# The first norm of a trunk layer: x loaded by features and scaled by a row, in place of normalizing by tokens and transposing

## The chip, the cores and the metric

The kernel runs on one core of one Trainium2 chip. The metric is the device time of one execution in microseconds (us). The engines are TensorE (PE in the profile; its weight loads are PEld), VectorE (DVE), ScalarE (ACT) and GpSimd (POOL); SyncE (SP) issues every DMA of this kernel, and they go through one queue.

## The reference

The layer is a pre-normed stick-breaking attention and a dense SwiGLU feed-forward on x of 2048 tokens by 1024 features in float32, with shift, scale and gate worked out from a vector c. What matters here is its very first step:

```python
def rms_norm(x, g):
    y = xf * lax.rsqrt(jnp.mean(xf * xf, axis=-1, keepdims=True) + EPS)
    return (y * g.astype(jnp.float32)).astype(x.dtype)
...
h = modulate(rms_norm(x, norm_g[i, 0]), sh_m, sc_m)     # h * (1 + scale) + shift
qkv = (h @ w_qkv).reshape(b, s, 3, N_HEADS, HEAD_DIM)
```

So h of a token t and a feature d is x[t, d] * rstd[t] * gain[d] + shift[d], with one rstd a token and one gain and shift a feature.

## The kernel before

Tokens are cut into four blocks of 512 (0 to 3), features into eight groups of 128 (k = 0 to 7). Attention heads are taken in eight pairs p. TensorE needs h with features on partitions, as tiles of 128 features by 512 tokens, each split into a high and a low part in float32r (the pair `ht`), because every product is three matmuls: high by high, high by low, low by high (`mm3`, lines 169 to 171). Three such matmuls are called a slice here; a projection of one block to q, k or v of a head pair is eight slices.

The norm before, for blocks 1 to 3: `x_load` brings four tiles of 128 tokens by 1024 features. `x_square` (line 160 does the square with its sum on ScalarE) and the helper's lines 162 (mean, VectorE) and 164 (power -1/2, GpSimd) give a scale for each token. `x_scale` (line 315, VectorE) multiplies a tile of x by it. `x_turn` (line 324) turns a feature group of the four tiles on TensorE into PSUM, a group of four 128x128 transposes. `modulate` then applies gain and shift out of PSUM on ScalarE (line 334), makes the high part on VectorE (line 340) and the low part (line 342) on VectorE for blocks 1 and 2 and on GpSimd for block 3. `first_norm` (line 361 on) does this for one k, and stores two groups of h to DRAM (`h_s`, line 363) for the later head pairs. Block 0 has its own code (lines 700 to 716) and isn't changed.

The order of the work around it is written out by hand. `project` yields once a slice. `STEPS` starts with (pair 0, block 0), then (pair 1, block 0), whose results are parked in DRAM ("parked"), then (pair 0, blocks 1, 2, 3). In each step the products come in the order k (t = 1), q (t = 0), v (t = 2). While a step runs, the next block's norm is prepared: its x is loaded in the k product, its squares and scales are done in the q product (`t == 0`), its first three feature groups in the v product (slices 2, 4 and 6); the other five are done in the first slices of its own k product, three ahead of use. From slice 42 of the projections on, the attention of the first blocks runs between the slices: scores z (line 528), sigmoids on ScalarE (545, 547), scans on VectorE (557, 562), weights by a multiplication on GpSimd (569), transposes t (579), copies aT (589 on ScalarE, 595 on VectorE), and products with v (607).

Each engine works its instructions in the order written. Only the order on SyncE is left to the framework, which places each DMA by its own reckoning of time. A DMA instruction on SyncE waits for the data, for a free buffer and for the DMA eight places ahead of it; what stands behind it waits too. Tiles share rings of buffers by tag: x in `v` (7 buffers), normalized x in `kt` (7, with the keys), h in `ht` (5), the intermediate `hf` in `tmp` (4). In the text, kt and qt are the copies of a block's keys and queries, `k_park` and `q_park` the parked ones, and wr a raw projection weight.

Of the kernel before, what the change touches and what calls it, by code (L numbers as in the profile page):

```python
# [9 lines left out]
F32 = mybir.dt.float32  # L10
F32R = mybir.dt.float32r
AF = mybir.ActivationFunctionType
# [57 lines left out]

H2_STEP = 3

LAST_HELD = 30

HOW = ["aav", "avv", "avv", "avp"]


def f32(ap):
    return ap.bitcast(F32)
# [22 lines left out]
def hybrid_trunk_kernel(  # L102
    ctx: ExitStack,
    tc: tile.TileContext,
    x: bass.AP,
    c: bass.AP,
    ada_first: bass.AP,
    ada_w: bass.AP,
# [79 lines left out]
    def load_weights(p, t, tag="wraw"):  # L188
        raw = att.tile([P, KC, P], F32, name=f"wr{p}_{t}", tag=tag, bufs=BUFS[tag])
        nc.sync.dma_start(raw, wqkv[p, t])  # L190
        raws[p, t] = raw
# [105 lines left out]
            yield  # L297


    x_tiles, x_norm, x_rstd = {}, {}, {}  # L300

    def x_load(b):
        for i in range(4):
            r0 = b * BT + i * P
            xt = att.tile([P, D], F32, name=f"x{b}_{i}", tag="v", bufs=BUFS["v"])
            nc.sync.dma_start(xt, x[r0 : r0 + P])
            x_tiles[b, i] = xt

    def x_square(b, i):
        xn = att.tile([P, D], F32, name=f"xn{b}_{i}", tag="kt", bufs=BUFS["kt"])  # L310
        x_norm[b, i] = xn
        x_rstd[b, i] = rms_scale(att, x_tiles[b, i], f"n0_{b}_{i}", junk=xn)

    def x_scale(b, i):
        nc.vector.tensor_scalar(
            x_norm[b, i], x_tiles.pop((b, i)), x_rstd.pop((b, i)), None, op0=ALU.mult
        )

    def x_turn(b, k):

        pool, tag = (tps, "t") if b < 2 else (accps, "acc")
        pt = pool.tile([P, BT], F32, name=f"xT{b}_{k}", tag=tag)
        for i in range(4):
            nc.tensor.transpose(
                pt[:, i * P : (i + 1) * P], x_norm[b, i][:, k * P : (k + 1) * P], ident
            )
        return pt

    def modulate(hl, pt, which, k, name, how="aap"):

        full = att.tile([P, BT], F32, name=name, tag="tmp", bufs=BUFS["tmp"])
        gain, add = g_eff[:, which, k : k + 1], shift[:, which, k : k + 1]
        if how[0] == "a":
            nc.scalar.activation(full, pt, AF.Identity, bias=add, scale=gain)
        else:
            nc.vector.tensor_scalar(full, pt, gain, add, op0=ALU.mult, op1=ALU.add)
        if how[1] == "a":
            nc.scalar.copy(hl[:, 0], full)
        else:
            nc.vector.tensor_copy(hl[:, 0], full)  # L340
        eng = nc.gpsimd if how[2] == "p" else nc.vector
        eng.tensor_tensor(hl[:, 1], full, f32(hl[:, 0]), op=ALU.subtract)

    def h_load(p, b):
        h = []
# [39 lines left out]
    def project(at):  # L385
# [10 lines left out]
        def product(t):  # L396
            if begun:
                return first_acc[t]
            w = weights[p, t]
            if parked and t == 1:  # L400
                acc = zps.tile([P, BT], F32, name=f"pj{p}_{b}_{t}", tag="z")
            else:
                acc = accps.tile([P, BT], F32, name=f"pj{p}_{b}_{t}", tag="acc")
            ahead = b == NB - 1 and p + 1 < NPAIR
            for k in range(KC):
                if t == 1:
                    if p == 0:
                        first_norm(b, k + 3)
                    if k == 0 and nb and nb > 1:
                        x_load(nb)  # L410
                    if k == 5 and waiting:
                        waiting.pop()()
                if parked and t == 1 and k % 2 == 0:
                    nc.sync.dma_start(*stores[k // 2])
# [12 lines left out]
            return acc  # L427
# [342 lines left out]
    for q in range(4):  # L770
# [835 lines left out]
```

## Time and profile before

| | |
|---|---|
| median of 3 runs | 2851.53 us (2848.06 to 2854.43) |
| the profiled execution | 2849.01 us |
| its span in the trace | 2846.9 us |
| outside the span | 2.1 us |
| granted TensorE clock | 1.0 |
| TensorE busy | 2797.7 us, 98% |

The changed stretch is the first 150 us of the span. Rows of the profile name an instruction by the line of the code that issues it and by the tiles it writes and reads (out<-in), with buffer numbers left out. A row of a timeline has the start, the duration, the engine, and in brackets how long the engine stood idle ahead of it and who ended that wait. A matmul's row is longer than the distance to the next one, since matmuls overlap in the array; distances of starts are used for costs. In the chain of waits each row is a start, a length and what the whole execution waited for at that moment.

### The profile page before, as it was taken

To read this page: it belongs to the slowest core of one execution; us is meant where nothing else is said; L and a number is where in the kernel's file an instruction comes from. 1 tells how busy PE (TensorE), PEld (TensorE's weight loads), DVE (VectorE), ACT (ScalarE), POOL (GpSimd) and SP (SyncE) were. 2 spreads that over 40 slices of the span, in tenths; PEclk is the share of its full clock that TensorE was granted. 3 is DMA by queue.
4 is the path that set the end of the run, shared out by engine and by line. 5 is a ranking of instruction groups with operands and counts; after the bars stand their busy time and mean duration, and the time that the engine had idled before them with its cause. 6 is when DMAs were issued, how large, how long until landed. Compare 5 with 4: busy or idle time off the path is not lost.

```text
span 2846.9 us, 41792 instructions
## 1 busy us (share of the span) xinstructions
PE 2797.7 (98%) x13848; PEld 2333.6 (82%) x13848; DVE 2031.8 (71%) x2825; ACT 1629.6 (57%) x3263; POOL 1278.3 (45%) x2032
## 2 busy tenths in 40 slices
PE   7999999999999999999999999999999999999998
PEld 6788888888888888887888888888788888888887
DVE  6788898888888888888866766555775665133477
ACT  4787877788787877777645533333433333322343
POOL 1475666666576655656410122221222222544454
PEclk9999999999999999999999999999999999999999
DMA  8765546656665635546289645334463335545565
GB/s 323 276 210 168 189 153 229 211 173 231 189 208 192 207 119 179 196 132 231 88 300 310 205 137 152 122 97 162 130 176 109 112 107 163 191 142 155 180 215 193
DMA packets 239368, 516.84 MB, mean 182 GB/s; under 512 B 22320, under 2 KB 110384, under 8 KB 221488
## 3 DMA queue, kind: packets, MB, share of 16 engines
q1 hardware_dynamic: 239152, 514.18, 55.7%
q8 instruction: 109, 1.79, 0.3%
q14 instruction: 107, 0.88, 0.1%
HBM read 346.85 MB, written 118.49 MB: 163 GB/s over the span
## 4 chain that ended last, share of the span: by engine, by line
PE 88%; DVE 5%; issue 2%; ACT 2%; DMA 1%; POOL 1%; SPq 0%; DVEq 0%; POOLq 0%; ACTq 0%
PE s L169 9%; PE s L171 9%; PE s L170 9%; PE z L528 8%; PE o L607 8%; PE t L579 8%; PE pj L169 6%; PE pj L170 6%; PE pj L171 6%; PE o L171 5%; PE o L169 5%; PE o L170 5%; PE y L171 1%; PE y L169 1%; PE y L170 1%
## 5 line engine op out<-in xcount | busy, mean ns | idle before, releaser
L569 POOL TENSOR_TENSOR a<-a,w 128x512 f32<-128x512 f32 (+3 forms) x640 | 620.0, 969 | 218.0 <-DVE w L562 127.1
L562 DVE TENSOR_TENSOR_SCAN w<-z,c,begin 128x512 f32<-128x512 f32 x384 | 489.4, 1279 | 82.0 <-ACT z L547 61.4
L169 PE MATMUL s<-r,l 128*128 128x512 f32 x1232 | 481.5, 391 | 4.3 <-DVE p L1369 3.9
L171 PE MATMUL s<-r,l 128*128 128x512 f32 x1232 | 479.5, 389 | 0.0
L170 PE MATMUL s<-r,l 128*128 128x512 f32 x1232 | 479.3, 389 | 0.0
L545 ACT ACTIVATE a<-z 128x512 f32<-128x512 f32 (+3 forms) x640 | 346.8, 542 | 167.4 <-PE z L528 137.1
L607 PE MATMUL o<-aT,v 128*128 128x512 f32 (+3 forms) x1280 | 384.2, 381 | 0.1
L595 DVE TENSOR_TENSOR aT<-t,aT 128x512 fp32r<-128x512 f32 (+3 forms) x640 | 358.9, 595 | 22.6 <-ACT aT L589 21.9
L528 PE MATMUL z<-kt,qt 128*128 128x512 f32 (+3 forms) x1280 | 363.1, 365 | 0.0
L589 ACT CAST aT<-t 128x512 fp32r<-128x512 f32 (+3 forms) x640 | 314.0, 533 | 73.8 <-PE t L579 63.6
L547 ACT ACTIVATE z<-z 128x512 f32<-128x512 f32 (+3 forms) x640 | 345.3, 539 | 0.0
L1377 POOL TENSOR_TENSOR one<-p,p 128x512 f32<-128x512 f32 x44 | 71.2, 1618 | 577.4 <-issue 320.3
L169 PE MATMUL pj<-ht,w 128*128 128x512 f32 x768 | 309.8, 403 | 6.3 <-issue 1.4
L170 PE MATMUL pj<-ht,w 128*128 128x512 f32 x768 | 302.2, 393 | 1.3 <-DVE ht L715 0.7
L579 PE MATMUL t<-begin,a 128*128 128x128 f32 x2176 | 294.8, 273 | 8.5 <-DVE aT L595 7.2
L579 PEld LDWEIGHTS t<-begin,a 128*128 128x128 f32 x2176 | 255.1, 140 | 58.1 <-DVE aT L595 11.0
L171 PE MATMUL pj<-ht,w 128*128 128x512 f32 x768 | 302.0, 393 | 0.0
L169 PEld LDWEIGHTS s<-r,l 128*128 128x128 f32 x1232 | 231.2, 188 | 54.5 <-ACT l L1230 2.9
L170 PEld LDWEIGHTS s<-r,l 128*128 128x128 f32 x1232 | 231.3, 188 | 48.5 <-issue 0.5
L171 PEld LDWEIGHTS s<-r,l 128*128 128x128 f32 x1232 | 231.2, 188 | 47.9
L557 DVE TENSOR_TENSOR_SCAN w<-z,begin 128x128 f32<-128x128 f32 (+3 forms) x256 | 208.7, 818 | 74.8 <-ACT z L547 63.3
L528 PEld LDWEIGHTS z<-kt,qt 128*128 128x128 f32 x1280 | 230.2, 188 | 37.4 <-DVE w L557 0.2
(160 smaller groups left out, 4866.5 us busy)
## 6 DMA issues: line engine op xcount, KB each, us to landing
ht<-h_s SPq DMA_DIRECT2D x108, 1024.0 KB, 8.0
wi<-in_win SPq DMA_DIRECT2D x86, 512.0 KB, 4.0
qt<-qn SPq DMA_DIRECT2D x124, 256.0 KB, 4.8
ol_qt<-act_s SPq DMA_DIRECT2D x56, 512.0 KB, 3.7
act_s<-S SPq DMA_DIRECT2D x66, 256.0 KB, 4.1
br<-in_wout SPq DMA_DIRECT2D x66, 256.0 KB, 3.6
h_s<-ht SPq DMA_DIRECT2D x16, 1024.0 KB, 7.9
o_s<-os SPq DMA_DIRECT2D x128, 128.0 KB, 2.7
```

The source lines that it names most:

```text
L169: nc.tensor.matmul(acc, lhs[0], rhs[0], start=first, stop=False, **kw)
L170: nc.tensor.matmul(acc, lhs[0], rhs[1], start=False, stop=False, **kw)
L171: nc.tensor.matmul(acc, lhs[1], rhs[0], start=False, stop=last, **kw)
L528: nc.tensor.matmul(z[:, :n], q[:, e, part, r * P : (r + 1) * P], k[:, e, :n], start=part == 0, stop=part == 1,)
L545: nc.scalar.activation(a[:, :n], z[:, :n], AF.Sigmoid, scale=QK_SCALE)
L547: nc.scalar.activation(z[:, :n], z[:, :n], AF.Sigmoid, scale=-QK_SCALE)
L562: nc.vector.tensor_tensor_scan(rest[:, rev], left[:, rev], begin[:, :BT][:, rev], initial=carries[r], op0=ALU.mult, op1=ALU.bypass,)
L569: nc.gpsimd.tensor_tensor(a[:, :n], a[:, :n], rest[:, 1 : n + 1], op=ALU.mult)
L579: nc.tensor.transpose(pt[:, rb * P : (rb + 1) * P], weighed[i, rb][:, j * P : (j + 1) * P], ident)
L589: nc.scalar.copy(hl[:, 0, t0:], pt[:, t0:])
L595: nc.vector.tensor_tensor(hl[:, 1, t0:], pt[:, t0:], f32(hl[:, 0, t0:]), op=ALU.subtract)
L607: nc.tensor.matmul(acc[:, t0:], lhs, hl[:, part, t0:], start=sc == qb and j == 0 and part == 0, stop=sc == 0 and j == 3 and part == 1,)
```

## The change

A second copy of x, laid out by features (`xt`: for blocks 1 to 3, 128 partitions of features, eight groups, 512 tokens), is passed to the kernel. It is made from the input on the host, as every other input's layout is. `cols_load` brings a block's columns in four tiles of 512 KB, in buffers of tag `kt`, where the normalized x lay. The token tiles of x are still loaded, but only for the squares. `x_spread` writes each token's scale 128 times into a 128x128 corner of its x tile; `x_share` turns these four corners on TensorE, which gives a tile with the row of 512 scales on every partition, and copies it to SBUF on ScalarE. `scale_cols` multiplies a feature group by the row, even k with the gain in one instruction on VectorE, odd k without it on GpSimd. `modulate` then adds the shift: for even k ScalarE writes the high part at once and VectorE the low part; for odd k ScalarE applies gain and shift, ScalarE copies the high part, and VectorE subtracts.

The places change too. Block 1's squares move from the parked step's q product to its k product, its row stands in the second slice of the parked q product, and four of its groups are done in the parked step (`NORM_AT`), at q slices 4 and 6 and v slices 3 and 5. Blocks 2 and 3 keep their squares in the q product, and their row stands ahead of the v product. The scaling runs two groups ahead of the modulation. The text calls block 1, 2 or 3 what the code calls `b`.

```diff
+NORM_AT = {True: [(0, 4), (0, 6), (2, 3), (2, 5)], False: [(2, 2), (2, 4), (2, 6)]}
...
+    def cols_load(b):
+        for m in range(KC // 2):
+            cols = att.tile([P, 2, BT], F32, name=f"xc{b}_{m}", tag="kt", bufs=BUFS["kt"])
+            nc.sync.dma_start(cols, xt[b - 1, :, 2 * m : 2 * m + 2])
+            x_cols[b, 2 * m], x_cols[b, 2 * m + 1] = cols[:, 0], cols[:, 1]
...
     def x_square(b, i):
+        if b > 0:
+            tok = x_tiles[b, i]
+            x_rstd[b, i] = rms_scale(att, tok, f"n0_{b}_{i}", junk=tok)
+            return
...
+    def x_spread(b, i):
+        nc.vector.tensor_scalar(
+            x_tiles[b, i][:, :P], ones, x_rstd.pop((b, i)), None, op0=ALU.mult
+        )
+
+    def x_share(b):
+        pool, tag = (tps, "t") if b < 2 else (accps, "acc")
+        pt = pool.tile([P, BT], F32, name=f"xr{b}", tag=tag)
+        for i in range(4):
+            tok = x_tiles.pop((b, i))
+            nc.tensor.transpose(pt[:, i * P : (i + 1) * P], tok[:, :P], ident)
+        x_row[b] = tok[:, BT:]
+        nc.scalar.copy(x_row[b], pt)
...
+    def scale_cols(b, k):
+        u = x_cols[b, k]
+        if k % 2 == 0:
+            nc.vector.scalar_tensor_tensor(
+                u, u, g_eff[:, 0, k : k + 1], x_row[b], op0=ALU.mult, op1=ALU.mult
+            )
         else:
+            nc.gpsimd.tensor_tensor(u, u, x_row[b], op=ALU.mult)
+
+    def modulate(hl, b, k):
+        u = x_cols.pop((b, k))
+        gain, add = g_eff[:, 0, k : k + 1], shift[:, 0, k : k + 1]
+        if k % 2 == 0:
+            nc.scalar.activation(hl[:, 0], u, AF.Identity, bias=add)
+            nc.vector.scalar_tensor_tensor(
+                hl[:, 1], u, add, f32(hl[:, 0]), op0=ALU.add, op1=ALU.subtract
+            )
         else:
+            nc.scalar.activation(u, u, AF.Identity, bias=add, scale=gain)
+            nc.scalar.copy(hl[:, 0], u)
+            nc.vector.tensor_tensor(hl[:, 1], u, f32(hl[:, 0]), op=ALU.subtract)
...
-        modulate(norm_h[b][k], x_turn(b, k), 0, k, f"hf{b}_{k}", HOW[b])
+        for ahead in range(0 if k == 0 else k + 2, min(k + 3, KC)):
+            scale_cols(b, ahead)
+        modulate(norm_h[b][k], b, k)
...
-                        first_norm(b, k + 3)
+                        first_norm(b, k + (4 if b == 1 else 3))
                     if k == 0 and nb and nb > 1:
                         x_load(nb)
+                        cols_load(nb)
...
-                if t == 0 and nb:
-                    (x_square if k < 4 else x_scale)(nb, k % 4)
-                if t == 2 and k in (2, 4, 6):
-                    first_norm(nb, k // 2 - 1)
+                if t == (1 if nb == 1 else 0) and nb:
+                    if k < 4:
+                        x_square(nb, k)
+                    if 2 <= k < 6:
+                        x_spread(nb, k - 2)
+                if nb and (t, k) == ((0, 1) if nb == 1 else (2, 0)):
+                    x_share(nb)
+                if (t, k) in NORM_AT[nb == 1]:
+                    first_norm(nb, NORM_AT[nb == 1].index((t, k)))
...
             load_weights(1, 2, "v")
+            cols_load(1)
```

More of the change, by code (lines that the diff above doesn't have):

```diff
@@ L105, in hybrid_trunk_kernel @@
     x: bass.AP,
+    xt: bass.AP,
     c: bass.AP,
@@ L297, in late_modulation @@
             yield
-    x_tiles, x_norm, x_rstd = {}, {}, {}
+    x_tiles, x_norm, x_rstd, x_cols, x_row = {}, {}, {}, {}, {}
     def x_load(b):
@@ L327, in x_turn @@
         return pt
[L329 to L334, printed above, removed]
-        else:
-            nc.vector.tensor_scalar(full, pt, gain, add, op0=ALU.mult, op1=ALU.add)
-        if how[1] == "a":
-            nc.scalar.copy(hl[:, 0], full)
-        else:
-            nc.vector.tensor_copy(hl[:, 0], full)
-        eng = nc.gpsimd if how[2] == "p" else nc.vector
-        eng.tensor_tensor(hl[:, 1], full, f32(hl[:, 0]), op=ALU.subtract)
+    def scale_cols(b, k):
[4 more added lines that the diff above has]
+            )
+        else:
+            nc.gpsimd.tensor_tensor(u, u, x_row[b], op=ALU.mult)
[7 more added lines that the diff above has]
+            )
+        else:
+            nc.scalar.activation(u, u, AF.Identity, bias=add, scale=gain)
+            nc.scalar.copy(hl[:, 0], u)
+            nc.vector.tensor_tensor(hl[:, 1], u, f32(hl[:, 0]), op=ALU.subtract)
     def h_load(p, b):
@@ L1581 @@
         "x": get("x")[0],
+        "xt": get("x")[0].reshape(NB, BT, KC, P).transpose(0, 3, 2, 1)[1:],
         "c": get("c")[0].reshape(KC, P).T,
```

10 lines of the change are left out of this document (4 added, 6 removed).

## The prediction, made before the changed kernel was run

> **What bounds the kernel now.** I read the page first, then the busy time in stretches, then the chain of waits over 50 to 150 us, then TensorE and the DMA issues one by one. The page, then five stretches (time, and busy us of PE, PEld, DVE, ACT and POOL, granted clock, DMA share, GB/s):
>
> ```profile
> span 2846.9 us, 41792 instructions
> PE 2797.7 (98%) x13848; PEld 2333.6 (82%) x13848; DVE 2031.8 (71%) x2825; ACT 1629.6 (57%) x3263; POOL 1278.3 (45%) x2032
> ...
> 45.00:50.00 5.00, 4.78 (x21) 3.49 (x20) 2.52 (x4) 4.60 (x6) 0.00 (x0) 1.00 0.01 5
> ...
> 80.00:90.00 10.00, 8.92 (x42) 6.96 (x41) 4.93 (x12) 5.32 (x10) 2.89 (x5) 1.00 1.02 395
> 90.00:100.00 10.00, 9.69 (x58) 8.04 (x57) 8.05 (x14) 8.04 (x18) 2.50 (x7) 1.00 1.04 295
> 140.00:150.00 10.00, 9.82 (x55) 7.73 (x54) 9.87 (x12) 8.59 (x17) 8.64 (x11) 1.00 0.57 200
> 150.00:160.00 10.00, 10.00 (x58) 8.67 (x57) 8.64 (x13) 8.48 (x18) 8.64 (x20) 1.00 0.97 321
> ```
>
> TensorE is the bound, and from 150 us on it shows no gap. So the change is worth what it moves the end of the third new block's norm, near 150 us; I take the 2700 us behind it as shifted whole. Ahead of that TensorE has gaps, and from 80 to 100 us all DMA engines are busy (from 45 to 50 they stood still). The chain of waits (start, us, what) names who makes the gaps:
>
> ```profile
> 76.03 7.69 DMA x<-in_x
> ...
> 106.48 0.59 ACT kn L431
> 107.07 1.04 ACT xn L160 x2
> 108.11 0.37 ACT aT L589
> ```
>
> For almost 8 us the chain of the whole kernel is the load of the third block of x (rows 1024 to 1535, "block 2"); it lands at 76.03 + 7.69 = 83.72, and TensorE waits for it. At 107 us it is ScalarE, which squares block 3 and only then serves the attention (aT).
>
> **What goes from TensorE.** Starts of TensorE work:
>
> ```profile
> 58.08 0.39 PE L169 MATMUL pj<-ht,w 128*128 128x512 f32 x1
> 58.76 0.39 PE L169 MATMUL pj<-ht,w 128*128 128x512 f32 x1
> 64.20 0.70 PE L324 MATMUL xT<-begin,xn 128*128 128x128 f32 x3
> 65.32 0.48 PE L169 MATMUL pj<-ht,w 128*128 128x512 f32 x1
> 70.46 0.60 PE L324 MATMUL xT<-begin,xn 128*128 128x128 f32 x4
> 71.60 0.60 PE L324 MATMUL xT<-begin,xn 128*128 128x128 f32 x4
> 85.82 0.33 PE L324 MATMUL xT<-begin,xn 128*128 128x128 f32 x1
> 87.89 0.47 PE L169 MATMUL pj<-ht,w 128*128 128x512 f32 x1
> 109.13 0.33 PE L579 MATMUL t<-begin,a 128*128 128x128 f32 x1 [0.16 <-DVE aT L595]
> 119.40 0.66 PE L324 MATMUL xT<-begin,xn 128*128 128x128 f32 x4 [1.04 <-DVE qn L432]
> 129.83 0.33 PE L579 MATMUL t<-begin,a 128*128 128x128 f32 x1 [0.54 <-DVE aT L595]
> 135.51 0.50 PE L169 MATMUL pj<-ht,w 128*128 128x512 f32 x1 [0.92 <-ACT hf L334]
> ```
>
> A slice of three products takes 58.76 - 58.08 = 0.68 us. With a group of four transposes in front it takes 71.60 - 70.46 = 1.14, so a group costs 0.46. Of 24 groups, three come back to turn the row of scales: 21 x 0.46 = 9.7 us of pure TensorE work go. Waits before the first group of a block: block 1, 65.32 - 64.20 - 0.46 = 0.66; block 2, 87.89 - 85.82 - 0.46 = 1.61; later 1.04, 0.54 and 0.92. All of it would be 14.4 us. The question is what is late next.
>
> **What the loads do.** DMA issues (start, us of the issue, count), then issues asked for singly (KB, us to landing):
>
> ```profile
> 33.96 0.33 SPq L414 DMA_DIRECT2D h_s<-ht  x1
> 55.83 1.28 SPq L462 DMA_DIRECT2D qt<-qn  x1
> 57.15 4.20 SPq L414 DMA_DIRECT2D h_s<-ht  x3
> 65.81 0.32 SPq L457 DMA_DIRECT2D q_park<-qn  x1
> 98.66 0.45 SPq L306 DMA_DIRECT2D x<-in_x  x1
> ```
>
> ```profile
> qt<-qn SPq DMA_DIRECT2D x1, 256.0 KB, 5.8
> ...
> q_park<-qn SPq DMA_DIRECT2D x1, 512.0 KB, 6.0
> ...
> x<-in_x SPq DMA_DIRECT2D x1, 512.0 KB, 7.8
> ```
>
> The last qt piece lands at 55.83 + 5.8 = 61.6, q_park at 65.81 + 6.0 = 71.8; between them went three stores of 1 MB and two of 0.5 MB: 4 MB in 10.2 us, 2.55 us per MB. The queue works in its order.
>
> The changed program, as built, reorders it. (a) Block 1's feature columns (2 MB) are issued behind the third product's weights and land by about 50 us, in the stretch where the DMAs stood still: free. (b) The first store of block 0's h, alone at 33.96 before, now stands behind kt and qt with the other three. So from 61.6 on the queue carries 4 MB of those stores, 1 MB of parked k and q, 2 MB of block 1's first two stores, and block 2's x (2 MB): 9 MB x 2.55 = 23.0, **x of block 2 lands at 84.6**, not earlier than the 83.7 of before, although it is issued some 5 us sooner. (c) Behind it stand 2 MB of block 2's columns (+5.1 us), while two weight loads (1 MB, -2.55) move far back. So block 3's first x, which landed at 98.66 + 7.8 = 106.5, comes at 106.5 + 0.9 + 5.1 - 2.55 = **109.9**. Also moved behind more data are kt and qt of block 1; by the same count qt lands near 102 to 103, where TensorE asks for it at about 105.
>
> **Prices of the new work.** Groups, mean ns:
>
> ```profile
> L334 ACT ACTIVATE hf<-xT,shift,g_eff 128x512 f32<-128x512 f32 x24 | 18.7, 779 | 16.3 <-PE xT L324 14.7 <-ACT z L547 1.0 <-ACT hf L334 0.6
> L160 ACT ACTIVATE xn<-x 128x1024 f32<-128x1024 f32 x12 | 12.7, 1060 | 0.9 <-DMA x<-in_x 0.7
> L569 POOL TENSOR_TENSOR a<-a,w 128x512 f32<-128x512 f32 x11 | 12.1, 1097 | 5.4 <-issue 4.2 <-DVE w L562 0.8
> L164 POOL TENSOR_TENSOR n_rstd<-n_ms,mhalf 128x1 f32<-128x1 f32 x12 | 8.3, 698 | 63.9 <-DVE n_ms L162 63.9
> ```
>
> ```profile
> L651 DVE SCALAR_TENSOR_TENSOR asum<-ac,c_act,asum 128x512 f32<-128x512 f32 x23 | 17.3, 750 | 1.0 <-DMA ac<-in_ada_first 0.4
> ...
> L710 ACT CAST ht<-hf 128x512 fp32r<-128x512 f32 x8 | 5.0, 620 | 0.3
> ```
>
> VectorE's scaling and low part with a scalar: 0.75 (L651). ScalarE out of SBUF: between 0.62 (L710, no bias) and 0.78 (L334, from PSUM); I take 0.62 plain, 0.70 with gain. Spreading a scale over 128x128 lies between nothing and L651's 0.75 for four times the width; I take 0.25, and as much for a sum's readout and its mean. GpSimd's scaling: 1.10 (L569). Per block VectorE does 4 + 8 instructions of some 0.75 and four spreads, about 10 us, as before; ScalarE 4 x 0.62 + 4 x (0.70 + 0.62) + 0.62 for the row, 8.4 for 6.2; GpSimd gets 4.4 us in blocks 1 and 2, and four multiplications for eight subtractions in block 3; it idles 5.4 us ahead of the attention's multiplications here (L569), which is the room for them. ScalarE's extra 2.2 us lie beside TensorE as long as ScalarE stays under its 8.6 of 10 us.
>
> **The sum, block by block** (after against before, at the same point of TensorE's order).
>
> *Block 1.* Its squares move ahead, right behind the copy of the first values, to about 52 to 57 us (4 x 1.06 + 0.25 each), and its row is turned in the second slice of the parked q product, which begins at 58.08: a wait of 0.3 at most. Four of eight tiles are ready before the k product of block 1 starts. TensorE gains 8 x 0.46 - 0.46 + 0.66 = 3.9. The v product of block 1 began two slices and a score pair (I take a group's 0.46) ahead of 85.82, at 84.0; now at 80.1.
>
> *Block 2.* Its row is now turned ahead of that product. x lands at 84.6; then square 1.06, power 0.70, and readout, mean, spread and the last transpose at 0.25 each: 2.8, so TensorE goes on at 87.4 after **7.3 us of waiting** in place of 1.6. Two slices and the score pair later it is at 89.2 where it was at 87.89: 1.3 late. The seven groups behind (3.2) put it ahead again: block 2's k product, before at its end when ScalarE took it up at 106.48, ends at 104.6 to 107.6, the 3 us for waits on VectorE, busy 8 of 10 there already.
>
> *Block 3.* That spread doesn't matter, because ScalarE's next work in order is block 3's first square, which now waits until 109.9 with the attention's copy aT queued behind it. VectorE's low part waits for that copy, and TensorE's fourth transpose group for its bank. Before, from that square (in the chain from 107.07, behind the copy kn) to that transpose (109.13) it took 2.1; now 109.9 + 2.1 = 112.0, **2.9 late**. Behind it go eight groups (3.7) and come one (0.46). Of the later waits I let 0.54 and 0.92 go (both stand behind the casts and the affine step out of PSUM), and the 1.04 come back as a wait for the row.
>
> Sum: 2.9 - 3.7 + 0.46 - 1.46 = **-1.8 us**. The profiled execution took 2849.01 us for its span of 2846.9, so it would take 2847.2; it lay 2.5 below the median of the runs shown, 2851.53, which goes to **2849.7**.
>
> **Rivals.** (1) *The loads are in time* (for it: x is issued earlier; against it: the queue is full from 57 us on). Then all 14.4 less some 0.5 for the new row waits: -13.9, 2837.6 against that median. (2) *Only block 3's x is in time*, if kt and qt go faster beside other transfers than by my count: it needs 3 us. Then block 2's k product, taken 1.2 ahead, keeps that: -1.2 - 3.7 + 0.46 - 1.46 = -5.9, 2845.6. (3) *Slower: VectorE and GpSimd block each other.* One row each:
>
> ```profile
> 99.74 1.47 DVE L342 TENSOR_TENSOR ht<-hf,ht 128x512 fp32r<-128x512 f32 x1
> 101.57 0.69 DVE L342 TENSOR_TENSOR ht<-hf,ht 128x512 fp32r<-128x512 f32 x1
> ```
>
> ```profile
> 99.52 1.13 POOL L569 TENSOR_TENSOR a<-a,w 128x512 f32<-128x512 f32 x1 [2.28 <-issue]
> ```
>
> The same VectorE subtraction takes 0.69 alone and 1.47 beside a GpSimd multiplication that it seems to wait out: 0.78 lost. After, twelve VectorE instructions a block read two tiles, and GpSimd multiplies beside them for the norm and the attention. If each loses 0.78, that is 9.4 a block. Block 2's part is mostly swallowed by the wait for x; block 3's is not. It decides from the third of the twelve on (1.8 / 0.78 = 2.3), and with eight of them hit it adds 6.2: +4.4, 2855.9; with all, 2859.1. [...]
>
> **How the numbers follow.** Forecast 0.42, (1) 0.18, (2) 0.14, (3) 0.26. About 0.2%, 5.7 us, is what a measurement of this kernel can tell from no change. Faster by more: all of (1), 0.09 of (2), 0.03 of the forecast, 0.30. Slower by more: 0.13 of (3), where ten or more are hit, and 0.05 of the forecast, 0.18. Within: 0.52. The forecast's own range is 2846 to 2854 (3 us for the landing of x, 2 for which waits go). With (1) down to its value and (3) but for its last step of 0.8, the range is 2837 to 2858.
>
> **What would show it.** Block 2's x landing at 83.5 to 86 us, and TensorE idle for 6 to 8 us ahead of the row's four transposes near 80 to 87; the chain of waits again on that load; ScalarE's first square of block 3 waiting for its x near 107 to 110; TensorE without gaps from 150 us on. Wrong: that idle time under 3 us (then rival 1); VectorE's two-input instructions near 1.1 us on average in 90 to 150 us (rival 3); a shift that still changes behind 160 us (then something beyond these blocks moved).

## The result, and the profile after

The changed kernel took 2857.21 us (median of 15 runs, 2854.76 to 2860.46) against 2849.28 for the kernel before in the same rounds: a ratio of **1.0024, 95% interval 1.0016 to 1.0032**, some 6.8 us slower by the ratio and 7.9 between the medians. The forecast was 1.8 us faster. The time lies inside the range that was given (2837 to 2858), in its last 0.8 us and on the other side of no change; the median of before that the forecast was counted from, 2851.53, lies 2.3 above this one. The range went that far for rival 3's sake, so that it holds the time says nothing for the sum.

The page after, and the same stretches as before (time, then busy us of PE, PEld, DVE, ACT, POOL, granted clock, DMA share, GB/s), with one more behind:

```profile
span 2856.8 us, 41649 instructions
PE 2797.1 (98%) x13764; PEld 2332.0 (82%) x13764; DVE 2041.5 (71%) x2821; ACT 1638.0 (57%) x3278; POOL 1292.7 (45%) x2036
...
80.00:90.00 10.00, 3.54 (x11) 2.30 (x10) 2.83 (x10) 5.66 (x10) 3.00 (x5) 0.69 1.03 414
90.00:100.00 10.00, 9.78 (x47) 7.71 (x46) 8.68 (x11) 7.52 (x16) 5.29 (x9) 0.96 1.01 365
100.00:110.00 10.00, 6.55 (x26) 5.13 (x26) 9.93 (x11) 6.70 (x14) 5.68 (x10) 0.83 0.98 360
140.00:150.00 10.00, 6.26 (x33) 4.71 (x32) 9.41 (x11) 8.74 (x17) 5.79 (x8) 0.94 0.66 237
150.00:160.00 10.00, 10.00 (x41) 8.30 (x40) 7.21 (x11) 7.32 (x18) 7.44 (x12) 0.72 0.52 178
```

The transposes are gone from TensorE: 13764 instructions for 13848, 84 fewer, 21 groups of four. Its busy time is hardly less all the same (2797.1 us of 2797.7), since a product at the lower clock counts longer: its row is 0.63 us from 89 to 90 us, at a granted 0.50, and 0.39 from 79 to 80, at 1.00. It now has large holes: 3.5 busy us of 10 in 80 to 90, 6.3 in 140 to 150, where it had 8.9 and 9.8. New is the column of the clock: 0.69, 0.83, 0.72, where it had been 1.00 from 40 us on.

The chain of waits, and the starts of TensorE's work that end a hole (last bracket: idle time before, and who ended it):

```profile
73.37 12.15 DMA x<-in_x
...
110.41 0.59 ACT kn L473
110.99 1.05 ACT x L160 x2
...
146.18 1.21 DVE ht L376
...
148.98 0.69 DVE aT L637
```

```profile
80.19 0.39 PE L171 MATMUL pj<-ht,w 128*128 128x512 f32 x1
85.94 0.45 PE L341 MATMUL xr<-begin,x 128*128 128x128 f32 x1 [5.36 <-DVE x L331]
...
101.22 0.50 PE L170 MATMUL pj<-ht,w 128*128 128x512 f32 x1 [1.13 <-DVE ht L376]
...
104.50 0.80 PE L170 MATMUL pj<-ht,w 128*128 128x512 f32 x1 [2.32 <-DVE ht L370]
```

```profile
141.78 0.63 PE L621 MATMUL t<-begin,a 128*128 128x128 f32 x4 [0.95 <-DVE aT L637]
...
149.71 0.90 PE L621 MATMUL t<-begin,a 128*128 128x128 f32 x3 [2.75 <-DVE aT L637]
```

Three places lose time. Block 2's x lands at 73.37 + 12.15 = 85.5, and TensorE, done with the product in front at 80.4, goes on with products at 88.25. Near 100 us it waits 1.13 and 2.32 us for VectorE's low parts of block 2. At 147 us it waits 2.75 us for aT, which VectorE makes only behind two low parts of block 3 (the chain's L376 at 146.18 and what follows).

How far TensorE is behind at each place is read by setting the start of one and the same product in both traces beside each other. The table gives that shift (us; minus is ahead) at five products of the kernel before and, at 144.9, an attention transpose ahead of the last wait of block 3, all named by their start there, for every kernel of this study, with the ratio of the whole time. At 54 us nothing has changed yet but for the start: subtract it. It is 2.7 and 2.4 us in the executions of f3_x2_early and f4_block1_x2_only. From 154 us on the shift stays within 0.1 us for 150 us and more; later, single executions scatter by a microsecond or two, and the ratio decides.

| kernel | 54.2 | 81.6 | 87.9 | 106.5 | 144.9 | 154.1 | ratio, 95% interval |
|---|---|---|---|---|---|---|---|
| changed | +0.1 | -3.6 | +3.1 | +3.9 | +1.7 | +7.1 | 1.0024 (1.0016 to 1.0032) |
| e1_stores_early | +0.1 | -1.7 | +2.2 | +3.1 | +0.8 | +6.3 | 1.0019 (1.0010 to 1.0028) |
| e2_scale_on_dve | +0.1 | -3.6 | +3.6 | +3.6 | +3.7 | +7.6 | 1.0035 (1.0022 to 1.0047) |
| e6_both | +0.5 | -3.2 | -1.2 | -0.1 | +1.0 | +4.9 | 1.0015 (1.0006 to 1.0024) |
| e3_warm | 0.0 | -3.7 | +3.7 | +4.6 | +2.4 | +6.4 | 1.0023 (1.0014 to 1.0032) |
| e8_warm2 | -0.3 | -4.0 | +2.5 | +2.7 | +0.9 | +6.3 | 1.0018 (1.0009 to 1.0027) |
| e4_block1 | +0.2 | -3.5 | +3.2 | +4.4 | +4.4 | +4.4 | 1.0018 (1.0009 to 1.0027) |
| e7_blocks12 | +0.2 | -3.6 | +3.8 | +4.7 | +4.7 | +4.7 | 1.0018 (1.0009 to 1.0027) |
| e5_block3 | +0.5 | +0.5 | +0.5 | +0.5 | -0.4 | +2.3 | 1.0012 (1.0003 to 1.0021) |
| f3_x2_early | +2.7 | -0.6 | -1.8 | -1.5 | -2.7 | 0.0 | 0.9994 (0.9986 to 1.0003) |
| g1_low3_pool | 0.0 | -2.1 | -3.3 | -3.2 | -3.5 | -1.2 | 0.9994 (0.9985 to 1.0003) |
| f1_block1_x2_early | +0.5 | -2.6 | -3.9 | -3.9 | -3.9 | -3.9 | 0.9985 (0.9976 to 0.9994) |
| f2_blocks12_x2_early | +0.4 | -2.2 | -3.4 | -2.5 | -2.5 | -2.5 | 0.9989 (0.9980 to 0.9998) |
| f0_loads_only | +0.2 | +0.2 | -1.2 | -1.1 | -1.2 | -1.2 | 0.9992 (0.9983 to 1.0001) |
| f4_block1_x2_only | +2.4 | -1.4 | -1.6 | -1.6 | +3.0 | +3.0 | 1.0007 (0.9998 to 1.0016) |
| h1_no_pool_scaling | +0.2 | -3.5 | -4.7 | -4.4 | -3.4 | -1.6 | 0.9983 (0.9974 to 0.9991) |
| h2_no_dve_scaling | +0.1 | -3.6 | -4.8 | -5.5 | -6.9 | -4.6 | 0.9983 (0.9973 to 0.9992) |

The changed kernel's row tells the story: 3.6 us ahead behind block 1, near the 3.9 forecast; that and more lost to the load of block 2's x; and in block 3, where the forecast won 4.7 us, another 3.2 lost.

### The profile page after: what moved, and what is told of

Same layout as the page of the kernel before. It is cut to its first block, busy times and chain, and to the rows that moved or that the text cites. A ratio compares the mean times of both kernels' runs of the same rounds, so it can differ in the third digit from the quotient of the medians.

```text
span 2856.8 us, 41649 instructions
## 1 busy us (share of the span) xinstructions
PE 2797.1 (98%) x13764; PEld 2332.0 (82%) x13764; DVE 2041.5 (71%) x2821; ACT 1638.0 (57%) x3278; POOL 1292.7 (45%) x2036
## 4 chain that ended last, share of the span: by engine, by line
PE 86%; DVE 5%; issue 3%; ACT 2%; DMA 2%; POOL 1%; SPq 0%; DVEq 0%; POOLq 0%; ACTq 0%
PE s L169 9%; PE s L170 9%; PE s L171 9%; PE z L570 8%; PE o L649 8%; PE t L621 8%; PE pj L169 6%; PE pj L170 6%; PE pj L171 6%; PE o L171 4%; PE o L169 4%; PE o L170 4%; PE y L171 2%; PE y L169 2%; PE y L170 2%
## 5 line engine op out<-in xcount | busy, mean ns | idle before, releaser
L631 ACT CAST aT<-t 128x512 fp32r<-128x512 f32 (+3 forms) x640 | 314.0, 533 | 72.8 <-PE t L621 62.7
```

The source lines that it names most:

```text
L631: nc.scalar.copy(hl[:, 0, t0:], pt[:, t0:])
```

## The experiments

Theory A, the forecast's own: the loads decide, the rest is won. Theory B: besides, VectorE's two-input instructions lose time beside GpSimd's (for short the port, a name for durations alone: 0.66 to 0.75 us or, beside a multiplication on GpSimd, up to 1.87 in the changed kernel), and TensorE's clock halves behind long waits (0.50 granted from 104.4 to 107.8 us there, behind the wait of 2.32). Theory C came after the first four: in block 3 VectorE is as full as TensorE, so that transposes taken from TensorE win nothing there.

### The loads, first attempt, and the scaling's engine

e1_stores_early, the store loop put behind block 0's norm in place of one store every second slice of the parked k product:

```diff
+    for store in stores:
+        nc.sync.dma_start(*store)
...
-                if parked and t == 1 and k % 2 == 0:
-                    nc.sync.dma_start(*stores[k // 2])
```

> The four stores of block 0's h (4 MB) go ahead of kt and qt of block 0, into the stretch from 47 us on in which the DMA queue runs empty in the changed kernel; nothing else changes. Both theories: block 2's x lands near 77 us in place of 85.5, and TensorE's wait of 7.2 us ahead of block 2's row (80.4 to 88.1) goes but for 1 us, with the half-speed stretch behind it. Theory A (the loads are all of it): the time then falls to that of my rival 1, 0.995 to 0.997 of the kernel before. Theory B (loads, and besides VectorE and GpSimd holding each other up, and a TensorE clock that halves behind each longer wait): the waits of TensorE for VectorE in blocks 2 and 3 stay, the one near 147 us above all (2.75 us and 2.6 us of half clock behind it); 0.998 to 1.001.

It missed under both: block 2's x landed at 84.5, one us earlier. The queue in front was empty, but SP stood at the store of block 1's second pair of tiles until 72.8 us, and the loads of x are issued behind it. The shorter queue didn't help a load that was issued late. The wait at the end of block 3 stayed at 2.76.

e2_scale_on_dve, and e6_both with e1's edit as well:

```diff
-            nc.gpsimd.tensor_tensor(u, u, x_row[b], op=ALU.mult)
+            nc.vector.tensor_tensor(u, u, x_row[b], op=ALU.mult)
```

> The odd tiles of blocks 1 to 3 are multiplied by the row on VectorE in place of GpSimd; the loads are as in the changed kernel. Theory B (the port): VectorE's two-input instructions of the norm fall from a mean of 1.0 to 1.1 us in 88 to 150 us to 0.75 to 0.85 (the attention's GpSimd multiplications still meet some), four instructions of 0.7 come per block, and the wait near 147 us shrinks from 2.75 to under 1.5 us: 2 to 4 us faster than the changed kernel, 1.001 of the kernel before. Rival (VectorE is simply overloaded, GpSimd's share was a relief): VectorE gets 2.8 us more per block and the waits grow: 2 to 5 us slower than the changed kernel, 1.003 to 1.004. The wait for block 2's x stays at 7 us under both.

> Both edits: the stores of block 0's h early, and the odd tiles scaled on VectorE. Theory B: neither the wait for x nor the port's share is left, the time falls to 0.996 to 0.998 of the kernel before, and lower than with either edit alone. Rival to B (VectorE simply overloaded): the same as the stores alone or slower than that by 2 to 4 us.

VectorE's groups in the norms of blocks 2 and 3 (count, busy us, mean ns), changed kernel, then e2_scale_on_dve:

```profile
L370 DVE SCALAR_TENSOR_TENSOR ht<-xc,shift,ht 128x512 fp32r<-128x512 f32 x8 | 8.5, 1068 | 0.1
L376 DVE TENSOR_TENSOR ht<-xc,ht 128x512 fp32r<-128x512 f32 x8 | 8.4, 1046 | 1.1 <-ACT ht L375 1.1
L358 DVE SCALAR_TENSOR_TENSOR xc<-xc,g_eff,x 128x512 f32<-128x512 f32 x8 | 7.9, 1004 | 0.7 <-ACT x L343 0.7
```

```profile
L358 DVE SCALAR_TENSOR_TENSOR xc<-xc,g_eff,x 128x512 f32<-128x512 f32 x8 | 7.3, 908 | 0.7 <-ACT x L343 0.7
L370 DVE SCALAR_TENSOR_TENSOR ht<-xc,shift,ht 128x512 fp32r<-128x512 f32 x8 | 6.9, 863 | 0.0
L376 DVE TENSOR_TENSOR ht<-xc,ht 128x512 fp32r<-128x512 f32 x8 | 6.5, 813 | 0.1
L362 DVE TENSOR_TENSOR xc<-xc,x 128x512 f32<-128x512 f32 x8 | 6.4, 802 | 0.0
```

The mean fell from 24.8 / 24 = 1.03 us to 27.1 / 32 = 0.85, as theory B has it, and yet it got no faster: 1.0035 for 1.0024, with intervals that overlap, and a shift of +7.6 for +7.1. Eight more instructions outweigh what the 24 gained, VectorE's sum rises by 2.3 us, as the rival has it. With the stores early as well (e6_both) it was 1.0015, inside the interval of e1_stores_early and far from the 0.996 to 0.998 expected; there block 2's x was also issued earlier, and landed at 73.67 + 7.79 = 81.5. Neither the load nor the port was the whole cause.

### The clock

e3_warm: 22 matmuls of 512 columns ahead of the row's first transpose. e8_warm2 fills between the transposes too:

```diff
+            if b == 2:
+                for _ in range((24, 8, 0, 6)[i]):
+                    nc.tensor.matmul(
+                        pt[:, i * P :], warm[0], warm[1][:, i * P :], start=True, stop=True
+                    )
             nc.tensor.transpose(pt[:, i * P : (i + 1) * P], tok[:, :P], ident)
```

> 22 matmuls of 128x512 into the row's own bank, which the row's transposes overwrite, are put ahead of block 2's row: TensorE works through 5 of the 7.2 us that it waits there. Nothing that the output needs changes. Theory of the clock (a wait of over 2 us is followed by some 3 us at half clock): the six products behind the row keep a pitch of 0.23 us in place of 0.43, and TensorE is 1.2 us earlier at the next score product; the granted clock in 80 to 90 us rises from 0.69 to 0.95 or more. At the end of block 3 between 0 and 1.2 us of it are left. Rival (the slow pitch comes from the loads or from the port, not from the wait): the pitch stays at 0.43.

> The changed kernel, with matmuls that fill the wait for block 2's x in full: 24 of 512 columns ahead of the row's first transpose, 8 of 384 columns ahead of the second, 6 of 128 ahead of the fourth, all into columns that the transposes behind them overwrite. (With 22 ahead of the first alone, waits of 0.8, 1.0 and 0.4 us were left within 3 us, and the pitch behind them was still 0.43.) Theory of the clock: without any wait of over 0.4 us the products behind the row come at a pitch of 0.23, and TensorE is 1.0 to 1.3 us earlier at 92 us than in the changed kernel, if the filling itself ends no later than the row's data. Rival (the slow pitch is not from the idle time): 0.43 again.

The starts of the products behind the row: the changed kernel, then e8_warm2.

```profile
88.25 0.77 PE L169 MATMUL pj<-ht,w 128*128 128x512 f32 x1
...
89.67 0.63 PE L169 MATMUL pj<-ht,w 128*128 128x512 f32 x1
90.10 0.63 PE L170 MATMUL pj<-ht,w 128*128 128x512 f32 x1
90.53 0.48 PE L171 MATMUL pj<-ht,w 128*128 128x512 f32 x1
90.84 0.33 PE L570 MATMUL z<-kt,qt 128*128 128x128 f32 x2
```

```profile
88.76 0.48 PE L169 MATMUL pj<-ht,w 128*128 128x512 f32 x1
...
89.54 0.39 PE L169 MATMUL pj<-ht,w 128*128 128x512 f32 x1
89.77 0.40 PE L170 MATMUL pj<-ht,w 128*128 128x512 f32 x1
90.00 0.39 PE L171 MATMUL pj<-ht,w 128*128 128x512 f32 x1
90.23 0.33 PE L575 MATMUL z<-kt,qt 128*128 128x128 f32 x2
```

A pitch of 0.43 in the one, 0.23 in the other. From the first product to the score product behind the six it took 90.84 - 88.25 = 2.59 in the changed kernel and 90.23 - 88.76 = 1.47 with the wait filled: **1.1 us was the clock's**, and it follows the idle time, not the loads or the port. e3_warm failed to show it: waits of 0.79, 0.97 and 0.42 us were left between its transposes, and the pitch was still 0.43. The whole gain is small (1.0018 against 1.0024, the intervals overlap), since filling doesn't bring x earlier.

### One block at a time

Blocks outside a set take the old path, x transposed and put through the affine step out of PSUM:

```diff
+NEW = {1}
...
-        modulate(norm_h[b][k], b, k)
+        if b in NEW:
+            modulate(norm_h[b][k], b, k)
+        else:
+            modulate_turned(norm_h[b][k], x_turn(b, k), k, f"hf{b}_{k}", HOW[b])
```

e4_block1 has {1}, e7_blocks12 {1, 2}, e5_block3 {3}.

> Only block 1 takes the new norm. All theories: TensorE is some 3.6 us ahead at 80 us, as in the changed kernel. The load theory: block 2's x lands no earlier than in the kernel before (83.7; the first store of h goes behind kt and qt as in the changed kernel, so 84 to 85), TensorE waits for it, and the lead is gone at 90 us: -0.5 to +1.5 at 155 us, 0.9998 to 1.0006. Rival (block 1's lead is kept): -3 to -4 us, 0.9987.

> Blocks 1 and 2 take the new norm, block 3 is as in the kernel before. Theory C: the shift of about +4 us that the changed kernel has at 113 us is carried through block 3 without growing and the wait of 2.75 us near 147 us is gone: +2.5 to +4.5 at 155 us, 1.0010 to 1.0015. Theory A: block 3's eight groups would be missed, +6 to +8 at 155 us, 1.002 to 1.003.

> Blocks 1 and 2 are as in the kernel before, only block 3 takes the new norm. Theory C (in block 3 VectorE is the bound: 9.9 of 10 us in 140 to 150 us in the kernel before, and the new norm gives it four scalings and eight subtractions where it had eight casts): nothing is won by the transposes that go, TensorE waits over 2 us near the end of block 3 and runs at half clock behind it, and the shift against the kernel before is near 0 at 113 us and +2 to +4 at 155 us; 1.0007 to 1.0015. Theory A (only the loads were at fault, and here they are nearly as before): the eight groups are won, -3 to -6 us, 0.998 to 0.999.

e4_block1 lost more than expected: the lead of 3.5 us runs into a wait of 6.7 us for the same x, which lands at 86.8 (before 83.7).

```profile
88.94 0.48 PE L354 MATMUL xT<-begin,xn 128*128 128x128 f32 x1 [6.70 <-DVE xn L329]
```

So block 1's norm, right by itself, comes out at +4.4; that the order of the changed kernel's loads is to blame (its columns in front, the first store of block 0's h behind kt and qt) is shown by f1_block1_x2_early below. e7_blocks12 carries its +4.7 through block 3 without a change, as theory C has it. e5_block3 loses 1.8 us from 106.5 to 154 us with nothing else changed, where theory A won 3 to 6. 1.3 are lost at block 3's first square, whose x lands at 99.17 + 9.56 = 108.7 (before 106.5); the second row is the wait at the end (the line numbers of these kernels are a little higher):

```profile
110.92 0.33 PE L647 MATMUL t<-begin,a 128*128 128x128 f32 x1 [1.45 <-DVE aT L663]
...
147.60 0.55 PE L647 MATMUL t<-begin,a 128*128 128x128 f32 x3 [2.76 <-DVE aT L663]
```

### The loads in time

f3_x2_early is the changed kernel with e1's edit and the four loads of block 2's x issued in the parked q product:

```diff
+                if parked and (t, k) == (0, 2):
+                    x_load(2)
...
                     if k == 0 and nb and nb > 1:
-                        x_load(nb)
+                        if nb > 2:
+                            x_load(nb)
                         cols_load(nb)
```

f1_block1_x2_early and f2_blocks12_x2_early do this with the sets {1} and {1, 2}, f0_loads_only with none, f4_block1_x2_only with {1} and without e1's edit.

> The changed kernel with the load of block 2's x really early: the four stores of block 0's h go ahead of kt and qt (as before), and the four loads of block 2's x are issued in the third slice of the parked q product, ahead of the stores of block 1's h. (With the stores alone early, the queue in front of x was empty, but SP reached the loads only behind the store of block 1's second pair of tiles, at 72.8 us, and x landed at 84.5.) x should land near 71 us and TensorE's wait ahead of block 2's row go wholly. If the load is all that was wrong (rival 1 of the prediction), the shift at 155 us is -8 or lower and the ratio 0.996 to 0.997. If VectorE bounds blocks 2 and 3 (theory C), the waits of 1.1, 2.3 and 2.76 us for VectorE stay and eat it: -3 to +1, 0.9990 to 1.0005.

> Only block 1 takes the new norm, with both load edits of f3_x2_early. The load theory: block 1's lead of 3.6 us is kept, and the kernel before's own wait of 1.6 us for block 2's x goes too: -4 to -5.5 at 95 us; what is left of it at 155 us depends on block 3's x: -3 to -5.5, 0.998 to 0.999. Rival (the lead runs into the next wait, for block 3's x or for VectorE in block 2): -2 to 0, 0.9993 to 1.0.

> The kernel before (no new norm in any block) with both load edits: what they bring by themselves. At most the wait of 1.6 us ahead of block 2's norm: -1.6 to 0 at 155 us, 0.9995 to 1.0. If it is much more, the loads and not the norm are what the other runs gain by.

> Blocks 1 and 2 with the new norm, block 3 as before, and both load edits. From f3_x2_early (-0.64 at 81.6 us, -1.48 at 106.5, +0.05 at 154) against f1_block1_x2_early (-2.56, -3.91, -3.93) block 2's new norm costs about 0.5 us and block 3's 1.5 us. If that holds, the shift goes from -2.5 at 81.6 us to -3.4 at 106.5 and stays there: 0.9985 to 0.9990. If block 2's is the dear one (its wait of 2.3 us for VectorE near 100 us): -1 to -2 at 155 us, 0.9993 or more.

> Only block 1 new, with block 2's x issued early, but the four stores of block 0's h left where the changed kernel has them, behind kt and qt. If the place of x behind block 1's stores was the fault, x lands near 79 us, in time for block 2's norm at 81, and the shift at 155 us is -3 to -4 as in f1_block1_x2_early (0.9985 to 0.9990). If the moved first store is the fault (1 MB, 2.55 us), x is 2 to 3 us late, TensorE waits, and the shift is -1 to +1.

In f3_x2_early x landed at 73.7 us and TensorE's longest single wait ahead of the row was 0.42 us. The ratio went from 1.0024 to 0.9994: **the loads' order was worth 0.0030 of the time, 8.5 us**, some of it perhaps not the loads but half clock behind the last wait of block 3, which cost 2.7 us in the changed kernel's profiled execution and nothing in this one. Rival 1 is refuted all the same: with the loads in time it said 13.9 us faster than before, and 1.7 came. Block 3's first x is still late here (it lands at 96.86 + 9.58 = 106.4, and TensorE waits 1.16 for what follows it, 0.16 before), but that is 1.0 us. The wait at the end of block 3 is the old one, here at full clock:

```profile
145.30 0.55 PE L622 MATMUL t<-begin,a 128*128 128x128 f32 x3 [2.76 <-DVE aT L638]
```

f1_block1_x2_early, the new norm in block 1 alone with the loads early, is **the kernel that beats both: 0.9985 (0.9976 to 0.9994)**, and its shift of -3.9 passes blocks 2 and 3 untouched. Of that the loads by themselves are 1.3 (f0_loads_only, whose interval still holds 1). Adding block 2 gives back 1.4 us (f2_blocks12_x2_early against f1, -2.5 for -3.9), in the waits of 1.14 and 2.31 us for VectorE; the expectation had 0.5. Adding block 3 gives back 1.5 between 106.5 and 154 us (f3_x2_early), 1.0 of it at block 3's first x. The shifts are of one execution each; the ratios of f1, f2 and f3 lie in this order, but their intervals overlap.

f4_block1_x2_only shows the forecast's chain most purely. Its x of block 2 lands at 82.1 and costs nothing more, but 4 MB of stores still stand in the queue, block 3's x lands at 99.14 + 10.83 = 109.97, and then:

```profile
99.14 10.83 DMA x<-in_x
...
109.99 1.15 ACT xn L164 x2
111.14 0.37 ACT aT L660
...
111.53 0.57 DVE aT L666
...
112.15 0.48 PE t L650
```

The load, ScalarE's square, the copy aT queued behind it, VectorE's part, the transpose at 112.15: 2.2 us behind the landing, and 4.79 us of waiting on TensorE. The forecast had 109.9, 2.1 and 112.0 for the changed kernel. The length of the chain is borne out; that the landing agrees to 0.1 us is luck, since this execution started 2.4 late. Without that start its shift at 154 is +0.6, in the range expected for the moved store, but the wait stands at block 3's x and not at block 2's. Neither edit was enough where it was tried alone (e1_stores_early with all three blocks, f4_block1_x2_only with block 1); of the two queue effects asked about, the place of x's loads decided block 2, and the stores in front of them decided block 3.

### What is left in blocks 2 and 3

g1_low3_pool moves block 3's odd low parts to GpSimd; h1_no_pool_scaling leaves out the odd tiles' scaling (GpSimd), h2_no_dve_scaling the even tiles' (VectorE), all three on top of f3_x2_early:

```diff
-            nc.vector.tensor_tensor(hl[:, 1], u, f32(hl[:, 0]), op=ALU.subtract)
+            eng = nc.gpsimd if b == 3 else nc.vector
+            eng.tensor_tensor(hl[:, 1], u, f32(hl[:, 0]), op=ALU.subtract)
```

```diff
-        else:
-            nc.gpsimd.tensor_tensor(u, u, x_row[b], op=ALU.mult)
```

> As f3_x2_early, and in block 3 the four odd tiles' low parts are subtracted on GpSimd in place of VectorE, which takes 4 x 0.7 us off VectorE between 120 and 150 us and puts 4 x 1.1 on GpSimd. Theory C (VectorE's own load is the bound there): the waits in block 3, 2.76 us at the end above all, shrink by 2 to 3 us against f3_x2_early. [...]

> As f3_x2_early, but the odd tiles of blocks 1 to 3 are not multiplied by the row at all: 12 GpSimd instructions are left out, and with them that part of the norm. VectorE keeps its instructions. Port theory: VectorE's two-input instructions of the norm, 0.9 to 1.07 us on average in f3_x2_early, fall to 0.8 to 0.85, and the waits of TensorE for VectorE in blocks 2 and 3 shrink by 2 to 4 us together: 0.9980 to 0.9988. Rival (VectorE's own load, or the order of its queue): means and waits as in f3_x2_early, within 1 us of it, 0.9992 to 0.9997.

> The counterpart: the even tiles are not multiplied (12 VectorE instructions left out, with that part of the norm), GpSimd's odd ones stay. VectorE's own load: 3 us less per block, the waits in blocks 2 and 3 shrink by 3 to 5 us, 0.9975 to 0.9985. Port theory alone: the eight low parts a block still meet GpSimd, means of 1.0 stay; 1 to 2 us, 0.9988 to 0.9992.

g1_low3_pool is undecided: the wait at the end of block 3 fell from 2.76 to 1.15 us as theory C has it, but one of 2.25 us near 128 us took its place, and the ratio is the same 0.9994. Taking work away gives 0.9983 on either side, against 0.9994: 3.1 us each, but the intervals overlap. h1_no_pool_scaling's VectorE, with its instructions unchanged:

```profile
L368 DVE SCALAR_TENSOR_TENSOR ht<-xc,shift,ht 128x512 fp32r<-128x512 f32 x8 | 7.6, 945 | 0.3
...
L374 DVE TENSOR_TENSOR ht<-xc,ht 128x512 fp32r<-128x512 f32 x8 | 6.3, 782 | 1.7 <-ACT ht L373 1.7
...
L358 DVE SCALAR_TENSOR_TENSOR xc<-xc,g_eff,x 128x512 f32<-128x512 f32 x6 | 4.9, 825 | 0.0
```

18.8 / 22 = 0.85 us, against (8.5 + 7.9 + 7.3) / 24 = 0.99 for the same instructions in f3_x2_early, on which it builds: that is what GpSimd's scaling adds to VectorE's durations. In TensorE's time the trace doesn't show it. TensorE's waits in block 3 of over 0.5 us add up to 7.6 us in h1 and to 7.5 in f3_x2_early: the last fell to 1.75 from 2.76, one near 129 us rose to 1.70 from 1.35, and the one for block 3's x to 1.90 from 1.16. Without the start, the shift at 154 is -1.9 in h1, -2.6 in f3_x2_early and -4.7 in h2. In h2_no_dve_scaling the low parts kept means of 1.09 and 1.14. Both are thus at work on VectorE, the port and its own number of instructions; TensorE's gain is seen in the trace for the second alone, and what the port costs the whole is not shown. In h1 the wait near 96 us was still 2.34 us, so that one is not GpSimd's scaling.

## Why the prediction was wrong, point by point

**What bounds the kernel.** "TensorE is the bound" was half of it. The row quoted there for 140 to 150 us has VectorE at 9.87 of 10 beside TensorE's 9.82. Both were full there, and the forecast took only one of them for the bound. Over the whole of block 3 VectorE wasn't full (34.8 of 40 us from 109 to 149 before, 36.9 of 43 from 113 to 156 after), so it is also a matter of what stands ahead of what in its queue.

**Block 1** was right: 3.9 forecast, 3.7 measured (-3.6, less the start of +0.1).

**The loads** were right: block 2's x at 84.6, measured 85.5; block 3's first x at 109.9, measured 110.2 (in the rows of f4_block1_x2_only 109.97). TensorE resumed at 88.25 for 87.4. The queue was not the only thing to hold block 2's x, though: with the queue in front of it empty it still landed at 84.5 (e1_stores_early), because it was issued late.

**Block 2.** The forecast put the shift at +1.3 at the product that starts at 87.89 before; measured +3.1. Of the missing 1.8, 0.85 is the later start of TensorE (88.25 for 87.4, with the landing 0.9 later). The other 1.0 is the halved clock, which the forecast didn't have: from there to that product it took 2.8 us, where the forecast counted 1.8. Then it let 3.2 us of transposes be won and wrote that the spread "doesn't matter", because ScalarE would wait for block 3's x next. It didn't: the waits of 1.13 and 2.32 us for VectorE delayed the k product so far that ScalarE came to block 3's square at 110.99, behind the copy kn, with x already there at 110.2. The shift was +3.9, not +2.9, by another route.

**Block 3 is the step that failed**: "Behind it go eight groups (3.7) and come one (0.46). Of the later waits I let 0.54 and 0.92 go", and so -4.7 from there to the end. Measured, from +3.9 to +7.1, is +3.2. The transposes went, 3.2 net, and the old waits with them (1.04, 0.54, 0.92, and 0.3 and 0.2 that the text didn't name, 3.0 together); in came waits of 0.73 for the row and 0.56, 1.35, 0.95 and 2.75 for VectorE, 6.3 together, and 2.7 of half clock: the shift grows by 5.4 from 144.9 to 149.4 in the changed kernel and by 2.7 in f3_x2_early, where the same wait ends at full clock. -3.2 - 3.0 + 6.3 + 2.7 = +2.8 of the 3.2. Three runs agree on what the new norm does in block 3 apart from the clock and from block 3's x: 3.2 - 2.7 in the changed kernel, 1.5 - 1.0 in f3_x2_early and 1.8 - 1.3 in e5_block3 are 0.5 us lost each, where the forecast won 4.7.

The forecast had written VectorE's work "about 10 us, as before" for every block, and then let the TensorE time that went count in full. In block 3 before it was eight casts, four scalings ahead of them and four means, 7.0 + 3.3 + 0.6 = 10.9 us; after it was four scalings, eight low parts with two inputs, four spreads and four means, 2.9 + 4.6 + 3.3 + 1.2 + 0.6 = 12.6. So VectorE got no less to do, but 1.7 us more, and the low parts stand in its queue ahead of the attention's aT, for which TensorE waits. VectorE, then GpSimd, at the end of block 3 in the changed kernel:

```profile
145.52 0.66 DVE L637 TENSOR_TENSOR aT<-t,aT 128x512 fp32r<-128x512 f32 x1
146.10 1.28 DVE L376 TENSOR_TENSOR ht<-xc,ht 128x512 fp32r<-128x512 f32 x1
147.31 1.75 DVE L370 SCALAR_TENSOR_TENSOR ht<-xc,shift,ht 128x512 fp32r<-128x512 f32 x1
148.98 0.68 DVE L637 TENSOR_TENSOR aT<-t,aT 128x512 fp32r<-128x512 f32 x1
```

```profile
145.75 1.09 POOL L611 TENSOR_TENSOR a<-a,w 128x512 f32<-128x512 f32 x1 [0.26 <-DVE w L604]
146.80 1.71 POOL L362 TENSOR_TENSOR xc<-xc,x 128x512 f32<-128x512 f32 x1
```

The two low parts take 1.28 and 1.75 us in place of 0.7 each, and each ends some 0.55 us behind a GpSimd instruction (145.75 + 1.09 = 146.84, 146.80 + 1.71 = 148.51), as if it did its own 0.7 only when that was done; aT comes behind them. In h1_no_pool_scaling, which hasn't the second of the two GpSimd instructions, the wait there was 1.75 in place of 2.75, though other waits of block 3 grew.

**Rival 3** came nearest: slower, 2855.9 to 2859.1, and its sign was there (two-input instructions at 1.0 to 1.05 us, where it named 1.1). Its reason is only a part: what can be had by taking GpSimd's scaling away is at most about 3 us by the ratio (h1_no_pool_scaling) and nothing by its trace, where the rival charged 6 to 9. That its number came near is in part luck: the clock and the order of VectorE's queue, which no rival had, made up the difference. Rivals 1 and 2 had the loads wrong (85.5 and 110.2 in the changed kernel), and f3_x2_early refutes the gains: with the loads nearly in time the change is even with the kernel before. A chance of 0.18 for slower was too little for a change that moves three engines' queues at once.

**The wait near 100 us** stays without GpSimd's scaling, and VectorE's rows in the changed kernel show what it is made of (TensorE's wait of 2.32 us ends at 104.50):

```profile
101.09 1.21 DVE L599 TENSOR_TENSOR_SCAN w<-z,begin 128x512 f32<-128x512 f32 x1
102.22 0.72 DVE L358 SCALAR_TENSOR_TENSOR xc<-xc,g_eff,x 128x512 f32<-128x512 f32 x1
102.87 1.58 DVE L370 SCALAR_TENSOR_TENSOR ht<-xc,shift,ht 128x512 fp32r<-128x512 f32 x1
```

The low part that TensorE needs stands behind the attention's scan and behind a scaling for a later group, and it ends 0.55 us behind the attention's own GpSimd multiplication (102.45 + 1.45 = 103.90), which it seems to wait out. In h2_no_dve_scaling, without that scaling, the low part took 0.72 us, and waits of 0.81, 0.19 and 0.73 us stood in the place of the 2.3.

**Left open**: whether another order of VectorE's queue brings this back with the scaling in place, and whether the clock's halving at the end of block 3 can be had back by filling that wait. Neither was tried.

## What to carry to other kernels

Ask for each stretch which engines are full, not which one is the bound, and what stands ahead of what in the queue of the engine that feeds it: here work taken from TensorE was won in block 1 and not in blocks 2 and 3. When a change adds or moves transfers, follow the issuing engine's order as well as the queue: here block 2's x landed at 85.5 us with the stores in front of it, at 84.5 without them, since its issuer stood at a store until 72.8, and at 73.7 with both edits. Look at the granted clock behind TensorE's waits: here half clock added 1.0 us behind the wait for block 2's x and 2.7 behind one of 2.75 in the changed kernel, and nothing behind 2.76 us in two others.

## What the runs showed of the hardware

**TensorE's clock.** From 40 to 160 us of the changed kernel the granted clock was 0.50 from 83.9 to 90.7 us, from 104.4 to 107.8 and from 148.7 to 155.6, for 6.8, 3.4 and 6.8 us, about waits of TensorE that ended at 85.94 (5.36 us long), 104.50 (2.32) and 149.71 (2.75). Stretches of one us (same columns as above):

```profile
83.00:84.00 1.00, 0.00 (x0) 0.00 (x0) 0.04 (x1) 1.00 (x2) 0.55 (x1) 0.94 1.05 430
...
90.00:91.00 1.00, 1.00 (x5) 0.77 (x5) 1.00 (x1) 0.00 (x0) 1.00 (x2) 0.65 1.00 422
...
148.00:149.00 1.00, 0.00 (x0) 0.00 (x0) 1.00 (x2) 0.46 (x1) 1.00 (x2) 0.86 0.91 385
149.00:150.00 1.00, 0.29 (x2) 0.29 (x3) 1.00 (x3) 0.97 (x3) 0.10 (x1) 0.50 0.98 401
...
154.00:155.00 1.00, 1.00 (x5) 0.90 (x4) 0.86 (x1) 0.51 (x2) 0.00 (x0) 0.50 0.66 270
155.00:156.00 1.00, 1.00 (x4) 0.73 (x4) 0.00 (x0) 1.00 (x3) 0.99 (x1) 0.72 0.00 0
```

The clock's mean of 0.94 and 0.65 in the first two of these rows, 0.68 and 0.62 in 104 to 105 and 107 to 108 us, and 0.86 and 0.72 in 148 to 149 and 155 to 156 give these ends; of the last 6.8 us six were fully busy. It is not a plain rule of the wait's length: 2.75 us brought it here and 2.76 in e1_stores_early, e3_warm and e8_warm2, the same 2.76 us in e5_block3 and f3_x2_early did not, and three waits of 0.4 to 1.0 us near 87 us in e3_warm, with only transposes between them, did. In e3_warm the half clock at the end of block 3 was over at 153.2, after some 3.4 us. What sets it off and how long it lasts is not shown beyond these figures.

**VectorE beside GpSimd.** In the changed kernel, from 88 to 152 us, the norms of blocks 2 and 3 have 24 two-input instructions on VectorE (L358, L370, L376). Ten of them ended 0.54 or 0.55 us behind a GpSimd multiplication and took 0.81 to 1.87 us; the other 14 took 0.66 to 0.75.

**The queue.** In the kernel before the store of h issued at 76.73 us landed 10.8 us later, at 87.5, and the DMA issued eight places behind it, a weight, was issued at 87.52. No DMA of that trace was issued ahead of the landing of the one eight places in front of it, and all landed in the order of their issue.
